# Where the low parts of the merge weights are subtracted, and how fast the convolution is handed out, in a two-layer hybrid block

## The chip, the cores and the metric

The kernel runs on one core of one Trainium2 chip. The metric is the device time of one execution in microseconds (us), as the median of several runs. The engines are TensorE (PE in the profile, its weight loads PEld), VectorE (DVE), ScalarE (ACT), GpSimd (POOL) and SyncE (SP, which here issues nearly all DMA transfers).

## What is computed

The reference is a transformer block of two layers on 1024 tokens of 1024 features, with 256 context tokens ahead of them that are updated in the first layer only. Per layer, one wide product `h @ w_in` yields the inputs of three branches (a: a gated convolution along the sequence, b: neighbourhood attention, c: window attention) and the merge gates. Each branch is gated, projected and weighed by its merge gate:

```python
def conv_branch(u_glu, u_gate, conv_w, conv_b, ln_g, ln_b, w_proj):
    a = u_glu[..., :D_CONV] * jax.nn.sigmoid(u_glu[..., D_CONV:])
    a = depthwise_conv(a, conv_w, conv_b)
    a = jax.nn.silu(layer_norm(a, ln_g, ln_b))
    return (a * jax.nn.silu(u_gate)) @ w_proj
...
    y_a = conv_branch(a_glu, a_gate, conv_w, conv_b, cln_g, cln_b, w_proj_a)
    y_b = (o_na * jax.nn.silu(n_gate)) @ w_proj_b
    y_c = (o_wa * jax.nn.silu(w_gate)) @ w_proj_c
    g_a, g_b, g_c = jnp.split(merge, 3, axis=-1)
    y = jax.nn.sigmoid(g_a) * y_a + jax.nn.sigmoid(g_b) * y_b + jax.nn.sigmoid(g_c) * y_c
    return y @ w_o
```

The depthwise convolution has 31 taps (`CONV_K`) on 512 channels (`D_CONV`). `w_in` has 3 x 1024 columns for the merge gates and 512 for the gate of each branch.

## The kernel before

Everything is held with features on the 128 partitions and tokens along the free axis. The tokens come in groups of 512, 512 and 256 (`GROUPS`; the last is the context). Layer 0 works on all three (`ngr` = 3), layer 1 on the first two. The inputs are 32-bit floats, and each product is made from a high and a low part of weights (`wf`) and of activations (`hh`, `hl`): `product` (L686) issues three matmuls per 128 rows of the contraction, high with high, high weights with the low part of the activations, low weights with the high part. A product over 1024 features is 24 matmuls.

**Weights.** `load_w` (L640) brings half a block, 128 x 512 elements: a DMA from SP into a raw tile `rf` (two of these), a copy on ScalarE for the high part (L649), and a subtraction `rf` less high part for the low part (L650) on the engine that it is given, POOL if nothing is said. `load_block` (L652) makes two halves. There are four tiles `wf`, which is two blocks: a new block can be written only when PE has left the block before the last.

**Stages of a layer.** Norms and input projections, then the attention with other work filled in between, then what is left of the merge gates, the gates of branch b, the projection of b, gates and projections of c and a, and the output pass with `w_o`. The stage of this change begins where the attention ends.

**Merge gates.** `merge_gates` (L881) goes through 24 weight blocks per layer (three branches, eight blocks each). For each block and group of tokens it makes one product into a bank of PSUM (`mg_ps`); ScalarE evicts it through Tanh into `mg_t` (L893) and sends it to DRAM from its own queue. At the end of a block, `merges.load` (L903) starts the load of the block after the next. A part of the first blocks runs within the attention. After it, `merges.wide` is set, the products alternate between two pools of banks, and `along` (L877) pulls the convolution beside them.

**Convolution and its norm.** `side_norm` lists four channel blocks of convolution on 1024 tokens (and four on 256 tokens in layer 0), then the layer norms of all groups in turns. `conv` (L734) is 31 taps on DVE in two chains, `cv_out` (L745, L752) and `cv_odd` (L755, L757), their sum (L759), and a store to DRAM (L760). `conv_norm` (L763) loads a group again (`ln_in`, L772), sums its four channel blocks on DVE (L776, L778), and has PE spread the sum over the partitions with a matrix of ones (L781); DVE subtracts the mean (L783) and adds the squares (L787); PE adds them up in narrow matmuls (L791); DVE makes the reciprocal root and POOL puts it on a diagonal (L799), PE spreads it (L802), DVE multiplies (L804), and the last multiplication (L811) ends the SiLU. `Pace` (L856) hands this generator out: each stretch of products adds its nominal time, multiplied with `SHARE[0]`, to a credit, and steps are taken while the credit lasts.

**Gates of b.** `gate_blocks` (L908) does four weight blocks with one product per group (`gt_ps`), Tanh on ScalarE (L831), a multiplication on DVE (L832), and the product with the branch's output on POOL, ScalarE and POOL (L842 to L844). The same `Pace` goes on beside it, and what it still holds is issued behind the gates (`norming.finish()`). Its weight blocks, and those of the projections, are loaded with the subtraction on POOL.

**What sets the order.** PE's order is the order in which the code issues its instructions (`manual_schedule` for PE). The orders of the other engines and of SP's queue are made by the framework's scheduler from the whole program; each engine then works in that order.

Of the kernel before, what the change touches and what calls it, by code (L numbers as in the profile page):

```python
# [24 lines left out]
NEG = -3.0e38  # L25
FILL_NS = (1975.0, 2300.0)
FIRST_NS = 8000.0
SHARE = (0.9, 0.6)
LOAD_AT = 0
SWITCH_NS = 0.0  # L30
BUILD_AT = ((0, 1), (0, 1))
# [19 lines left out]
def hybrid_block_kernel(  # L51
# [9 lines left out]
    nc = tc.nc  # L61
# [581 lines left out]
    def load_w(src, pw, eng=nc.gpsimd):  # L643

        n = src.shape[1]
        raw = pw.tile([128, 4, 128], F32, tag="rf", bufs=RF, name="rf")
        nc.sync.dma_start(out=raw[:, 0:n, :], in_=src)
        w = pw.tile([128, 2, 4, 128], F32R, tag="wf", bufs=WF, name="wf")
        nc.scalar.activation(w[:, 0, 0:n, :], raw[:, 0:n, :], AF.Copy)  # L649
        eng.tensor_tensor(w[:, 1, 0:n, :], raw[:, 0:n, :], f32(w[:, 0, 0:n, :]), ALU.subtract)  # L650
        return w

    def load_block(src, pw, eng=(nc.gpsimd, nc.gpsimd)):
        return chunks_of([load_w(src[:, 4 * i:4 * i + 4, :], pw, eng[i]) for i in range(2)])
# [34 lines left out]
    def product(w, kn, hx, n, ps):  # L689

        hh, hl = hx
        for k in range(kn):
            for i, (b, a) in enumerate(((0, hh), (0, hl), (1, hh))):
                nc.tensor.matmul(  # L694
                    ps[:, 0:n], lhsT=w(k, b), rhs=a[:, k, 0:n],
                    start=(k == 0 and i == 0), stop=(k == kn - 1 and i == 2),
                )
            if k < kn - 1:
                yield 3 * max(n / 2.4, 107)

    def chunks_of(ws):
        return lambda k, b: ws[k // 4][:, b, k % 4, :]

    def mm_tile(name):
        return ps_mm.tile([128, 512], F32, tag="mm", name=name)
# [3 lines left out]
    def s_tile(name):  # L709
        flip[0] ^= 1  # L710
        if flip[0]:
            return ps_s.tile([128, 1024], F32, tag="s", name=name)
        return ps_t.tile([128, 1024], F32, tag="t", name=name)
# [143 lines left out]
    J0 = {"a": 12, "b": 20, "c": 28}  # L857
# [19 lines left out]
    def along(gen, side):  # L877
        for ns in gen:
            side.pull(ns)

    def merge_gates(l, h, pw, ngr, merges):  # L881


        flip = 0
        while merges.ready:
            br, f, w = merges.ready.pop(0)
            for gi in range(ngr):
                o, n = GROUPS[gi]
                flip ^= 1
                ps = s_tile("mg_ps") if merges.wide and flip else mm_tile("mg_ps")  # L890
                yield from product(w, KC, h[gi], n, ps)
                t = pw.tile([128, 512], F32, tag="t", bufs=3, name="mg_t")
                nc.scalar.activation(t[:, 0:n], ps[:, 0:n], AF.Tanh, scale=0.5)  # L893
                nc.scalar.dma_start(out=mg_d[br][f][:, o:o + n], in_=t[:, 0:n])
                yield 3 * max(n / 2.4, 107)
            merges.load(l, pw)

    class Merges:
# [4 lines left out]
        def load(self, l, pw):  # L903
            if self.todo:
                br, f = self.todo.pop(0)
                self.ready.append((br, f, load_block(wF[l, J0[br] + f], pw)))

    def gate_blocks(l, br, h, pw, px, og, ngr, side):  # L908

# [121 lines left out]
    def side_pool(l, nm, left):  # L1031
        return tc.tile_pool(name=f"{nm}{l}", bufs=1, reuse_waits="tile", side="left" if left == (l == 0) else "right")
# [45 lines left out]
    for l in range(L):  # L1078
# [7 lines left out]
        def end_fill():  # L1086
            spa.close()
            pools["pw"] = sw.enter_context(side_pool(l, "pw", True))
            pools["mg"] = merge_gates(l, h, pools["pw"], ngr, merges)
            merges.load(l, pools["pw"])  # L1090
            merges.load(l, pools["pw"])
            yield END_NS
# [7 lines left out]
        def side_norm():  # L1100
            for c in range(4):
                yield from conv(l, 0, S, c, lc, pools["pc"])
                if ngr == 3:
                    yield from conv(l, S, T, c, lc, pools["pc"])
            yield from in_turns(conv_norm(l, gi, lc, pools["pc"]) for gi in range(ngr))
# [5 lines left out]
        pw = pools["pw"]  # L1111
# [3 lines left out]
        with side_pool(l, "pc", True) as pools["pc"]:  # L1115
            norming = Pace(side_norm(), SHARE[0])
            along(pools["mg"], norming)
# [11 lines left out]
        if l + 1 < L:  # L1129
            cols += [(l + 1, lc_next, j) for j in range(0, 16, 2)]  # L1130
        side = Pace(ada_blocks(cols, px), SHARE[1])
        for br in "bca":
# [144 lines left out]
```

## Time and profile before

| what | value |
|---|---|
| runs | 2892.89, 2867.36, 2889.42 us |
| median | 2889.42 us |
| profiled execution, its own time | 2886.43 us |
| its span, first to last instruction | 2884.6 us |
| mean granted clock of TensorE | 0.98 |
| PE busy in the span | 2722.3 us (94%) |
| DVE, ACT, POOL busy | 1740.0, 1144.6, 1304.2 us |

The profile is of one execution; times in its views are counted from the start of the span. The stage of the change lies at 744.74 to 1100.85 us in layer 0 and at 2242.74 to 2496.40 us in layer 1, and the gates of b right behind it, to 1157 and to 2544 us. "Busy" counts an engine's own work and no waiting. The time in brackets behind a row is the idle time of the engine just ahead of it, with the instruction that released it. The granted clock is a share of TensorE's full speed.

### The profile page before, as it was taken

The numbers are of one execution on the slowest core, as the hardware profiler recorded it, in microseconds if no ns is written. First come the engines' busy times: TensorE is split into PE (matmuls) and PEld (weight loads), VectorE is DVE, ScalarE is ACT, GpSimd is POOL, SyncE is SP. The second block draws the span as 40 slices with busy tenths as digits, with TensorE's granted clock in tenths as the row PEclk, the third lists the DMA queues.
The fourth block names the chain that finished last, engine by engine and source line by source line (L and its number), as shares of the span: only waits on it lengthen the run. The fifth ranks groups of instructions, "written<-read, shape, count | busy, mean of one in ns | idle before, by whom it ended". The sixth has DMA issues, their size and how long they took to land. (4 is left out here: it accounts for less than half of the span.)

```text
span 2884.6 us, 43940 instructions
## 1 busy us (share of the span) xinstructions
PE 2722.3 (94%) x15060; PEld 2361.9 (82%) x15060; DVE 1740.0 (60%) x3676; ACT 1144.6 (40%) x2524; POOL 1304.2 (45%) x1330
## 2 busy tenths in 40 slices
PE   7999999999888999999998899999999995999999
PEld 4899989998777888888877899989888784777877
DVE  5577777766798713786355456677665896441132
ACT  3366666665311124121233356655555221412221
POOL 2333465533565515265645233466334325346652
PEclk9999999999999999999999999999999997999999
DMA  7445442221223323644354455452221332363345
GB/s 240 126 137 149 126 136 67 71 57 48 72 96 130 106 79 118 196 150 133 108 180 157 117 145 158 135 143 71 73 65 63 125 112 87 103 186 107 106 120 175
DMA packets 331664, 344.20 MB, mean 119 GB/s; under 512 B 82224, under 2 KB 249264, under 8 KB 331440
## 3 DMA queue, kind: packets, MB, share of 16 engines
q1 hardware_dynamic: 314160, 313.07, 36.6%
q10 hardware_dynamic: 17280, 28.32, 2.6%
q8 instruction: 119, 1.95, 0.3%
q14 instruction: 105, 0.86, 0.1%
HBM read 250.83 MB, written 90.44 MB: 118 GB/s over the span
## 5 line engine op out<-in xcount | busy, mean ns | idle before, releaser
L650 POOL TENSOR_TENSOR wf<-rf,wf 128x512 fp32r<-128x512 f32 x248 | 479.4, 1937 | 553.1 <-ACT wf L649 538.2
L694 PE MATMUL mg_ps<-hh,wf 128*128 128x512 f32 (+1 forms) x1920 | 574.5, 379 | 60.0 <-POOL wf L650 59.3
L342 PE MATMUL u_ps<-wu,hh 128*128 128x384 f32 (+2 forms) x1920 | 498.9, 342 | 11.4 <-DVE vr L370 3.9
L694 PEld LDWEIGHTS mg_ps<-hh,wf 128*128 128x128 f32 x1920 | 350.2, 190 | 132.6 <-POOL wf L650 62.3
L588 POOL TENSOR_SCALAR p<-p,rd 128x640 f32<-128x640 f32 (+1 forms) x288 | 215.8, 750 | 395.6 <-DVE rd L586 245.4
L694 PE MATMUL mg_ps<-hl,wf 128*128 128x512 f32 (+1 forms) x960 | 358.6, 374 | 0.0
L649 ACT ACTIVATE wf<-rf 128x512 fp32r<-128x512 f32 x272 | 170.4, 627 | 462.1 <-PE pp_ps L694 181.5
L342 PEld LDWEIGHTS u_ps<-wu,hh 128*128 128x128 f32 x1920 | 328.1, 191 | 17.3 <-ACT hh L281 4.7
L342 PE MATMUL u_ps<-wu,hl 128*128 128x384 f32 (+2 forms) x960 | 322.0, 335 | 1.5 <-DVE hl L282 1.2
L580 ACT ACTIVATE p<-p,nmx 128x641 f32<-128x641 f32 (+3 forms) x288 | 222.2, 772 | 245.7 <-DVE nmx L576 122.4
L694 PE MATMUL pp_ps<-ogh,wf 128*128 128x512 f32 (+1 forms) x960 | 282.1, 375 | 5.3 <-DVE mg_in L943 4.0
L694 PE MATMUL gt_ps<-hh,wf 128*128 128x512 f32 (+1 forms) x960 | 280.0, 374 | 5.8 <-DVE mg_in L943 3.4
L598 DVE TENSOR_TENSOR pt<-tp,pt 128x640 fp32r<-128x640 f32 (+1 forms) x288 | 215.8, 749 | 104.8 <-ACT pt L597 101.8
L752 DVE SCALAR_TENSOR_TENSOR cv_out<-cv_in,lc_conv_w,cv_out 128x1024 f32<-128x1024 f32 (+1 forms) x192 | 213.9, 1118 | 0.0
L694 PE MATMUL wo_ps<-hh,wf 128*128 128x512 f32 (+1 forms) x640 | 195.1, 387 | 19.7 <-DVE mg_in L943 7.5
L694 PEld LDWEIGHTS pp_ps<-ogh,wf 128*128 128x128 f32 x960 | 175.3, 189 | 43.3 <-DVE mg_in L943 6.6
L694 PEld LDWEIGHTS mg_ps<-hl,wf 128*128 128x128 f32 x960 | 181.9, 190 | 34.0 <-issue 1.4
L694 PEld LDWEIGHTS gt_ps<-hh,wf 128*128 128x128 f32 x960 | 174.6, 188 | 42.5 <-issue 3.9
L594 PE MATMUL tp<-ident,p 128*128 128x128 f32 x1280 | 187.4, 273 | 14.0 <-DVE pt L598 11.0
L626 POOL TENSOR_TENSOR ob<-cb_b,cb_e 64x256 f32<-64x256 f32 x144 | 106.3, 738 | 200.3 <-ACT cb_e L620 199.8
L597 ACT ACTIVATE pt<-tp 128x640 fp32r<-128x640 f32 (+1 forms) x288 | 181.8, 631 | 17.2 <-PE tp L594 15.1
L594 PEld LDWEIGHTS tp<-ident,p 128*128 128x128 f32 x1280 | 153.6, 140 | 41.1 <-POOL p L588 10.8
(165 smaller groups left out, 5443.1 us busy)
## 6 DMA issues: line engine op xcount, KB each, us to landing
rf<-in_wF SPq DMA_DIRECT2D x144, 256.0 KB, 2.7
rf<-in_wO SPq DMA_DIRECT2D x80, 256.0 KB, 2.9
ru<-in_wU SPq DMA_DIRECT2D x96, 192.0 KB, 3.3
bias<-in_na_bias SPq DMA_DIRECT2D x96, 192.0 KB, 2.6
w_ada_s<-in_w_ada SPq DMA_DIRECT2D x64, 256.0 KB, 3.1
nrm<-qk_d SPq DMA_DIRECT2D x40, 320.0 KB, 3.9
rf<-in_wP SPq DMA_DIRECT2D x48, 256.0 KB, 2.7
v_d<-vr SPq DMA_DIRECT2D x80, 128.0 KB, 2.1
```

What stands on the lines that cost most here:

```text
L342: nc.tensor.matmul(ps[:, c0:UW], lhsT=a[:, k, off * 128:(off + 1) * 128], rhs=ws[k][:, b, c0:UW], start=(k == 0 and i == 0), stop=(k == KC ...
L580: nc.scalar.activation(self.p[:, 0:n], self.p[:, 0:n], AF.Exp, bias=m, scale=1.0 if sink is None else -1.0, accum_out=self.den)
L588: nc.gpsimd.tensor_scalar(p, p, rd, 1.0, ALU.mult, ALU.mult)
L594: nc.tensor.transpose(tp[:, c * 128:(c + 1) * 128], self.p[:, c * 128:(c + 1) * 128], ident)
L597: nc.scalar.activation(self.pt[:, 0:nch, 0, :], tv, AF.Copy)
L598: nc.vector.tensor_tensor(self.pt[:, 0:nch, 1, :], tv, f32(self.pt[:, 0:nch, 0, :]), ALU.subtract)
L626: nc.gpsimd.tensor_tensor(o, b, e, ALU.add)
L649: nc.scalar.activation(w[:, 0, 0:n, :], raw[:, 0:n, :], AF.Copy)
L650: eng.tensor_tensor(w[:, 1, 0:n, :], raw[:, 0:n, :], f32(w[:, 0, 0:n, :]), ALU.subtract)
L694: nc.tensor.matmul(ps[:, 0:n], lhsT=w(k, b), rhs=a[:, k, 0:n], start=(k == 0 and i == 0), stop=(k == kn - 1 and i == 2),)
L752: nc.vector.scalar_tensor_tensor(r, a[:, k:k + n], tap, r, ALU.mult, ALU.add)
```

## The change

`SHARE[0]` goes from 0.9 to 0.8: the convolution and its norms are handed out more slowly against PE's nominal time. In `Merges.load`, blocks that are loaded once `wide` is set, so behind the attention, have their low parts subtracted on VectorE and no more on GpSimd. The weight blocks of the gates, projections and output pass are loaded as before.

```diff
-SHARE = (0.9, 0.6)
+SHARE = (0.8, 0.6)
...
         def load(self, l, pw):
             if self.todo:
                 br, f = self.todo.pop(0)
-                self.ready.append((br, f, load_block(wF[l, J0[br] + f], pw)))
+                eng = nc.vector if self.wide else nc.gpsimd
+                self.ready.append((br, f, load_block(wF[l, J0[br] + f], pw, (eng, eng))))
```

A blank line in `merge_gates` shifts later line numbers by one, and `load` by one more, so that L943 becomes L945.

**DVE, layer 0, merge stage.** The rows of before, some way into the first wide convolution:

```order
L752 SCALAR_TENSOR_TENSOR cv_out<-cv_in,lc_conv_w_400,cv_out 128x1024
L757 SCALAR_TENSOR_TENSOR cv_odd<-cv_in,lc_conv_w_400,cv_odd 128x1024
L752 SCALAR_TENSOR_TENSOR cv_out<-cv_in,lc_conv_w_400,cv_out 128x1024
L757 SCALAR_TENSOR_TENSOR cv_odd<-cv_in,lc_conv_w_400,cv_odd 128x1024
L752 SCALAR_TENSOR_TENSOR cv_out<-cv_in,lc_conv_w_400,cv_out 128x1024
```

The taps of the two chains alternate, and no subtraction stands among them. The rows now, from the first half of one weight block to the first half of the next:

```order
L650 TENSOR_TENSOR wf<-rf,wf 128x512
L752 SCALAR_TENSOR_TENSOR cv_out<-cv_in,lc_conv_w_400,cv_out 128x1024
L650 TENSOR_TENSOR wf<-rf,wf 128x512
L752 SCALAR_TENSOR_TENSOR cv_out<-cv_in,lc_conv_w_400,cv_out 128x1024
L757 SCALAR_TENSOR_TENSOR cv_odd<-cv_in,lc_conv_w_400,cv_odd 128x1024
L752 SCALAR_TENSOR_TENSOR cv_out<-cv_in,lc_conv_w_400,cv_out 128x1024
L757 SCALAR_TENSOR_TENSOR cv_odd<-cv_in,lc_conv_w_400,cv_odd 128x1024
L752 SCALAR_TENSOR_TENSOR cv_out<-cv_in,lc_conv_w_400,cv_out 128x1024
L757 SCALAR_TENSOR_TENSOR cv_odd<-cv_in,lc_conv_w_400,cv_odd 128x1024
L752 SCALAR_TENSOR_TENSOR cv_out<-cv_in,lc_conv_w_400,cv_out 128x1024
L757 SCALAR_TENSOR_TENSOR cv_odd<-cv_in,lc_conv_w_400,cv_odd 128x1024
L752 SCALAR_TENSOR_TENSOR cv_out<-cv_in,lc_conv_w_400,cv_out 128x1024
```

After these the next `L650` row follows. The two subtractions of a block have come into DVE's order, with one tap between them and nine behind them. The pattern holds through the stage of both layers with 8 to 10 wide taps a round in most rounds.

**PE, layer 0, start of the gates of b.** Before, no layer-norm matmul stands there:

```order
L694 MATMUL gt_ps<-hh_418,wf 128x512
L694 MATMUL gt_ps<-hl_419,wf 128x512
L694 MATMUL gt_ps<-hh_418,wf 128x512 x2
L694 MATMUL gt_ps<-hl_419,wf 128x512
L694 MATMUL gt_ps<-hh_418,wf 128x512 x2
L694 MATMUL gt_ps<-hl_419,wf 128x512
L694 MATMUL gt_ps<-hh_418,wf 128x512 x2
```

And now, from the same row on:

```order
L694 MATMUL gt_ps<-hh_418,wf 128x512
L694 MATMUL gt_ps<-hl_419,wf 128x512
L694 MATMUL gt_ps<-hh_418,wf 128x512 x2
L694 MATMUL gt_ps<-hl_419,wf 128x512
L694 MATMUL gt_ps<-hh_418,wf 128x512 x2
L694 MATMUL gt_ps<-hl_419,wf 128x512
L694 MATMUL gt_ps<-hh_418,wf 128x512
L781 MATMUL ln_ps<-ln_s,ones 128x512
L694 MATMUL gt_ps<-hh_418,wf 128x512
```

The first layer-norm matmul of layer 0 has moved from the merge stage to behind the first nine matmuls of the gates; the other sets follow it within the gates, nine in all in layer 0. In layer 1, two sets of L781 and one of L791 move there, and all six now stand in the gates.

**DVE, layer 1, end of the gates of b.** `L832` takes a gate's result; `L811` is the last step of the layer norm. The rows before:

```order
L804 TENSOR_TENSOR ln_in<-ln_in,ln_pr 128x512 x4
L832 SCALAR_TENSOR_TENSOR gt_t<-gt_t,gt_ps 128x512
L811 SCALAR_TENSOR_TENSOR ln_in<-ln_s,ln_in 128x512 x6
L832 SCALAR_TENSOR_TENSOR gt_t<-gt_t,gt_ps 128x512
L811 SCALAR_TENSOR_TENSOR ln_in<-ln_s,ln_in 128x512 x2
L832 SCALAR_TENSOR_TENSOR gt_t<-gt_t,gt_ps 128x512 x5
```

Five of the eight gate results come behind the layer norm's last step. The rows now:

```order
L804 TENSOR_TENSOR ln_in<-ln_in,ln_pr 128x512 x4
L832 SCALAR_TENSOR_TENSOR gt_t<-gt_t,gt_ps 128x512
L804 TENSOR_TENSOR ln_in<-ln_in,ln_pr 128x512 x4
L811 SCALAR_TENSOR_TENSOR ln_in<-ln_s,ln_in 128x512
L832 SCALAR_TENSOR_TENSOR gt_t<-gt_t,gt_ps 128x512
L811 SCALAR_TENSOR_TENSOR ln_in<-ln_s,ln_in 128x512 x6
L832 SCALAR_TENSOR_TENSOR gt_t<-gt_t,gt_ps 128x512
L811 SCALAR_TENSOR_TENSOR ln_in<-ln_s,ln_in 128x512
```

The last `L832` of the gates stands behind six multiplications of the layer norm. The layer norm's end has moved from the third result of the gates to the eighth.

## Rows read from the trace of the kernel before

**Rows 1.** The page, busy time of the engines

```profile
PE 2722.3 (94%) x15060; PEld 2361.9 (82%) x15060; DVE 1740.0 (60%) x3676; ACT 1144.6 (40%) x2524; POOL 1304.2 (45%) x1330
```

**Rows 2.** The page, costliest groups: columns are busy, mean ns, idle before

```profile
L650 POOL TENSOR_TENSOR wf<-rf,wf 128x512 fp32r<-128x512 f32 x248 | 479.4, 1937 | 553.1 <-ACT wf L649 538.2
```

**Rows 3.** Groups of line L650 on DVE: ns min/median/max

```profile
L650 DVE TENSOR_TENSOR wf<-rf,wf x24: 675/691/1643, 1508.2 to 2870.2; 128x512 fp32r<-128x512 f32 x24
```

**Rows 4.** POOL in order of time, quiet parts of both merge stages

```profile
1009.31 1.29 POOL L650 TENSOR_TENSOR wf<-rf,wf 128x512 fp32r<-128x512 f32 x1 [9.93 <-ACT wf L649]
...
1023.31 1.29 POOL L650 TENSOR_TENSOR wf<-rf,wf 128x512 fp32r<-128x512 f32 x1 [11.09 <-ACT wf L649]
...
2447.33 1.29 POOL L650 TENSOR_TENSOR wf<-rf,wf 128x512 fp32r<-128x512 f32 x1 [6.67 <-ACT wf L649]
...
2458.53 1.29 POOL L650 TENSOR_TENSOR wf<-rf,wf 128x512 fp32r<-128x512 f32 x1 [6.67 <-ACT wf L649]
```

**Rows 5.** Table by stretch: merge stage, gates of b; layer 0, then layer 1

```profile
core 0: us, PE busy (x) PEld busy (x) DVE busy (x) ACT busy (x) POOL busy (x), PEclk, DMA share, GB/s
744.74:1100.85 356.11, 328.95 (x1663) 274.73 (x1662) 259.10 (x353) 75.57 (x138) 171.50 (x56) 0.96 0.30 99
1100.85:1157.00 56.15, 56.15 (x291) 47.35 (x290) 15.25 (x21) 21.81 (x43) 34.34 (x29) 1.00 0.38 121
2242.74:2496.40 253.66, 222.47 (x950) 178.19 (x949) 187.89 (x160) 50.41 (x87) 94.50 (x40) 0.94 0.32 106
2496.40:2544.00 47.60, 47.60 (x207) 37.85 (x205) 23.07 (x45) 22.43 (x39) 29.31 (x29) 1.00 0.41 126
```

**Rows 6.** L650 on POOL in layer 0's merge stage, and who waited for it

```profile
L650 POOL TENSOR_TENSOR wf<-rf,wf x44: 1278/1517/26275, 752.0 to 1084.9; 128x512 fp32r<-128x512 f32 x44
...
  PE mg_ps L694: 26.8, 4
```

**Rows 7.** The same in layer 1's merge stage

```profile
L650 POOL TENSOR_TENSOR wf<-rf,wf x39: 1274/1368/33838, 2246.4 to 2493.8; 128x512 fp32r<-128x512 f32 x39
...
  PE mg_ps L694: 31.2, 1
```

**Rows 8.** PE in order of time, the two longest stalls

```profile
844.62 1.22 PE L694 MATMUL mg_ps<-hh,wf 128*128 128x512 f32 x2 [11.26 <-POOL wf L650]
...
2425.75 1.22 PE L694 MATMUL mg_ps<-hh,wf 128*128 128x512 f32 x2 [31.19 <-POOL wf L650]
```

**Rows 9.** POOL in order of time, the two longest pairs

```profile
818.29 28.49 POOL L650 TENSOR_TENSOR wf<-rf,wf 128x512 fp32r<-128x512 f32 x2 [8.35 <-ACT wf L649]
...
2391.85 35.52 POOL L650 TENSOR_TENSOR wf<-rf,wf 128x512 fp32r<-128x512 f32 x2 [17.00 <-ACT wf L649]
```

**Rows 10.** DVE in order of time, layer 0's merge stage

```profile
754.26 2.31 DVE L752 SCALAR_TENSOR_TENSOR cv_out<-cv_in,lc_conv_w,cv_out 128x1024 f32<-128x1024 f32 x1
756.49 1.27 DVE L757 SCALAR_TENSOR_TENSOR cv_odd<-cv_in,lc_conv_w,cv_odd 128x1024 f32<-128x1024 f32 x1
757.68 1.27 DVE L752 SCALAR_TENSOR_TENSOR cv_out<-cv_in,lc_conv_w,cv_out 128x1024 f32<-128x1024 f32 x1
...
797.38 0.47 DVE L757 SCALAR_TENSOR_TENSOR cv_odd<-cv_in,lc_conv_w,cv_odd 128x256 f32<-128x256 f32 x1
797.77 0.47 DVE L752 SCALAR_TENSOR_TENSOR cv_out<-cv_in,lc_conv_w,cv_out 128x256 f32<-128x256 f32 x1
...
1061.91 2.48 DVE L783 SCALAR_TENSOR_TENSOR ln_in<-ln_ps,ln_in 128x512 f32<-128x512 f32 x4 [61.50 <-PE ln_ps L781]
```

**Rows 11.** PE in order of time, layer-norm matmuls in layer 1's merge stage

```profile
2481.37 1.02 PE L781 MATMUL ln_ps<-ln_s,ones 128*128 128x512 f32 x2
...
2482.46 0.39 PE L694 MATMUL mg_ps<-hl,wf 128*128 128x512 f32 x1
...
2494.99 0.95 PE L791 MATMUL ln_ps<-ones,ln_s 128*128 128x1 f32 x8
```

**Rows 12.** DVE in order of time, gates of b in layer 1

```profile
2517.16 3.36 DVE L811 SCALAR_TENSOR_TENSOR ln_in<-ln_s,ln_in 128x512 f32<-128x512 f32 x4 [0.67 <-ACT ln_s L810]
```

## Prediction

> **What bounds the kernel now.** I read the page's totals first. TensorE is busy in 2722.3 of 2884.6 us [rows 1], so time can be won only where TensorE stands still or runs slowly. The costliest group of the page is then the subtraction of the low parts on GpSimd (POOL): 248 of them, 1937 ns each in the mean [rows 2]. The same subtraction takes 0.69 us on VectorE (DVE) where the output pass of this kernel has it there [rows 3], and 1.29 us on POOL where DVE does nothing beside it [rows 4]. So a mean of 1.94 us on POOL must hold some that are far longer.
>
> The table by stretch shows where [rows 5]. The four stretches are, in both layers, what is left of the merge stage after the attention, and the gates of branch b behind it. Layer 0's merge stage takes 356.11 us with PE busy in 328.95 at a granted clock of 0.96, layer 1's 253.66 us with 222.47 busy at 0.94. The gates of b are at full clock and never idle. The waits on the subtraction in these stretches come to 26.8 us in four places in layer 0 and 31.2 us in one place in layer 1, with single subtractions of up to 26.3 and 33.8 us [rows 6, 7]. PE's order of time shows the largest two, 11.26 and 31.19 us, each released by POOL [rows 8]. POOL's order of time shows what happened ahead of them: a pair of subtractions took 28.49 us, another 35.52 us, where a quiet one takes 1.29 [rows 4, 9].
>
> Beside them DVE does the convolution's taps back to back: 1.27 us each, begun 1.19 us apart, and 2.31 us for some that meet a subtraction [rows 10]. All engines but POOL and DVE are idle or light there, so I read a long subtraction as POOL kept out by an unbroken run of taps. DVE has no need of that haste. It has finished its part in layer 0 so early that it waits 61.50 us for PE's first mean of the layer norm [rows 10].
>
> **The change, part by part.** *The low parts move to DVE.* Some 42 subtractions in layer 0 and 36 in layer 1 leave POOL, which then has nothing to do in the merge stage. A weight block is two of them, 24 products per group of tokens. On DVE they cost 2 x 0.61 us of its time per block (0.69 long, taken to overlap its neighbour by the 0.08 us that taps do).
>
> What they meet there decides. DVE works in order, so a subtraction stands behind taps, and taps behind it wait while it waits. A block's buffer comes free when PE leaves the block, the high part follows, and the block is wanted one whole block later. The quiet pairs are 14.00 us apart in layer 0 and 11.20 us in layer 1 [rows 4]: that is PE's time per block, 72 matmuls there and 48 here. From these, a matmul of 512 columns takes 11.20/48 = 0.233 us, and one of 256 takes (14.00 - 11.20)/24 = 0.117.
>
> In the new order 9 taps stand between two pairs and 1 inside a pair. With 1.19 us per wide tap, 0.40 per narrow tap [rows 10] and 0.61 per subtraction, I count 16 rounds of 13.0 to 14.5 us in layer 0, 13.76 in the mean, and 16 rounds of 10.7 us in the mean in layer 1. Both are just under PE's 14.00 and 11.20. DVE is therefore paced by PE, and each pair is ready some 3 us after its buffer is free, 8 to 11 us before PE wants it. In layer 0 the taps run out after these 16 rounds and the last four pairs follow with nothing between. Where the taps were, the subtractions lie beside PE's work, so their cost is nothing; the cover is gone if the taps stretch, which is the third rival.
>
> *What PE gets back.* Layer 0: 22 blocks of 14.00 us, and 45 matmuls (21 of 512 columns, 24 of 256: 7.7 us) are 315.7 us. Nine layer-norm steps of PE stand in that stage, three kinds for three groups. A step of 512 columns costs PE 2482.46 - 2481.37 less the one product between, 0.86 us, and a step of eight small matmuls, recorded with 0.95, some 0.90 by the same reckoning [rows 11]. The narrow group is put at half. That makes 2 x (0.86 + 0.86 + 0.43) for the first and third kind and 0.90 + 0.90 + 0.45 for the second, 6.55 us. Stalls are 26.84. [...] Gain 26.84 + 7.0 = 33.8 us.
>
> Layer 1: 19.5 blocks of 11.20 are 218.4 us, layer-norm steps in that stage 2 x 0.86 + 0.90 = 2.62, stall 31.19; 253.66 less these leaves 1.45 us of low clock. Gain 31.19 + 1.45 = 32.6 us.
>
> *The share of 0.8.* PE's layer-norm matmuls move from the merge stage to the gates of b, all nine sets in layer 0 and three more, so all six, in layer 1. Their PE time moves with them (6.55 and 2.62 us) and nets out to nothing. New is that they are interleaved with gate products, whose results DVE also takes. Layer 1 shows what three such sets do there now: 47.60 us with no idle PE against 192 x 0.233 = 44.8, and 2.6 of layer norm, so 0.1 us per set. By hand, from the durations above, I find no stall of PE in layer 0's gates. In layer 1 the last result of the gates stands behind six multiplications of 0.84 us (four took 3.36 [rows 12]), 5 us of DVE's time, where none stood ahead of it before; by hand, 2.3 us of it are not covered and hold up the projection's first matmuls. From below this costs nothing; from above it is the first rival.
>
> *DMAs.* The weight loads are queued on SP, where the convolution's stores and the layer norm's loads stand too. In the new order a store waits for its last tap, and behind it stand loads whose buffers are freed by a later subtraction anyway; I charge nothing. If one of these did come late by what the longest such wait of DVE costs, the 8 us of lead would take most of it; 5 us per layer is my upper end.
>
> **The sum.** 33.8 + 32.6 - 2.3 = 64.1 us off 2886.43, the profiled execution's own time (its span is 2884.6): 2822 us. That execution is 3 us under the median, 2889.42, so this is 0.977 of the median.
>
> [...] The row is that a subtraction of 1.29 us took up to 33.8 us beside taps of 1.27 us, while many others took little more than 1.3 (median 1.37) [rows 7]. [...]
>
> **The rivals.** *First, the gates give it back.* In the gates of b, DVE must now serve 15 layer-norm sets between the results it takes from PE's two banks. The price at the top is one round of four subtractions of the mean per set, 2.48 us [rows 10]: 15 x 2.48 = 37 us, so 2822 + 37 = 2859. For it: both kinds of result are queued in one order on DVE. Against it: layer 1's three sets stand there now with no PE idle. Chance 0.11.
>
> *Second, no gain: the stalls come from the raw loads.* POOL's pair ahead of layer 1's stall began after 17.00 us of waiting for ScalarE's high part, where 6.67 is usual [rows 4, 9]. If late loads are the cause, the move only changes who waits. Then the 58 us remain and it takes 2886. Against it: those two subtractions then took 35.52 us of their own. Chance 0.05.
>
> *Third, slower: DVE becomes the pacer.* Taps and subtractions now share one order, at 98 and 96% of PE's time per block, 16 x 13.76 + 16 x 10.7 = 391 us against 16 x (14.00 + 11.20) = 403. Should DVE need f times as long, PE is held once 391 f exceeds 403 and the two leads of 11 and 8 us: beyond f = 1.08. At f = 1.24 the whole gain is gone. If every second tap took 2.31 us, as beside POOL now [rows 10], taps (352 of the 391) would grow by 1.43, and the excess is 352 x 1.43 + 39 - 422 = 120 us: 2822 + 120 = 2942. Against it: POOL, which stretches the taps today, has no work in this stage then. Chance 0.03.
>
> **How the numbers follow.** The forecast has 0.81. Its own range is 2803 to 2842: down by what the clock behind small waits elsewhere might give and the spread of an execution (0.3%, 9 us), up by 5 us per layer of late transfers and a half of the gates' price in layer 1. The first rival reaches to 2859, and I set the upper end at 2852, which takes in most of it. Left out are the other two and a part of the first, under 2 in 10 in all. A measurement of this kernel tells about 1% from no change, so faster means under 2860.5 and slower over 2918.3. Faster: 0.81 and all but 0.01 of the first rival, 0.91. Slower: the third, 0.03. Within 1%: the rest, 0.06.
>
> **What would show it.** Right: POOL has no subtraction in the merge stage; each on DVE lasts 0.7 us; PE idles under 3 us there in either layer, at a clock of 0.99 or more; the stage takes some 316 and 218.5 us; the gates of b take 63 us in layer 0 and 50 in layer 1. Wrong: waits of PE on subtractions of DVE; taps in the merge stage still longer than 1.3 us; gates of b over 66 us; or any stall of PE whose releaser is a raw load.

## The result and the profile after

On the chip of the first comparison the changed kernel takes 2840.02 us (2838.72 to 2844.24 in 4 runs) against 2887.77 of the kernel before: a ratio of 0.985, interval 0.980 to 0.990. On a second chip, beside other kernels, it takes 2837.29 against 2902.17, ratio 0.978 (0.976 to 0.980). It is faster, by 48 us in the first case and 65 in the second, where the prediction had 2822 us and a gain of 64. The profiled execution of the changed kernel took 2840.45 us with a span of 2838.6; it is 18.1 us over the forecast span of 2884.6 - 64.1 = 2820.5. The median of 2840.02 us lies inside the forecast range, 2 us under its upper end of 2842.

Where these are is read from the table by stretch of the changed kernel, with the boundaries at the same events as in [rows 5] and one stretch more, from layer 1's projection of b to its output pass (the columns are those of [rows 5]):

```profile
core 0: us, PE busy (x) PEld busy (x) DVE busy (x) ACT busy (x) POOL busy (x), PEclk, DMA share, GB/s
748.30:1065.20 316.90, 316.90 (x1631) 267.12 (x1630) 231.54 (x324) 62.22 (x114) 3.78 (x5) 1.00 0.34 110
1065.20:1133.85 68.65, 64.58 (x322) 52.77 (x322) 47.48 (x92) 34.33 (x65) 36.81 (x38) 0.98 0.29 95
2223.60:2441.80 218.20, 218.20 (x937) 175.52 (x936) 177.27 (x179) 46.07 (x79) 4.61 (x4) 1.00 0.37 123
2441.80:2492.50 50.70, 50.35 (x218) 39.35 (x217) 28.72 (x56) 24.19 (x41) 28.04 (x28) 1.00 0.26 78
2492.50:2742.40 249.90, 231.70 (x977) 184.32 (x976) 77.17 (x118) 55.40 (x94) 135.87 (x106) 0.98 0.46 137
```

Both merge stages have lost their stalls: PE is busy in every microsecond, at a clock of 1.00 where it was 0.96 and 0.94. POOL is left with 4 us of work in each. The gates of b have grown from 56.15 to 68.65 us, and there PE is not busy for 4.07 us of them. Set against the kernel before and the forecast, in us:

| stretch | before | forecast | after | after less forecast |
|---|---|---|---|---|
| merge stage, layer 0 | 356.1 | 315.7 | 316.9 | +1.2 |
| gates of b, layer 0 | 56.1 | 62.7 | 68.65 | +6.0 |
| merge stage, layer 1 | 253.7 | 218.4 | 218.2 | -0.2 |
| gates of b, layer 1 | 47.6 | 50.2 | 50.7 | +0.5 |
| from there to the output pass, layer 1 | 244.5 | 246.8 | 249.9 | +3.1 |
| all other stretches | 1926.6 | 1926.6 | 1934.2 | +7.6 |

The last row is work that the change doesn't touch. In the twelve profiled executions of this study the opening stretch alone took 142.3 to 146.5 us, the attention of layer 0 601.6 to 605.1 and layer 0's output pass 215.9 to 218.9, whatever was changed, and the execution of the changed kernel shown here drew high numbers in two of the three. So of 18 us some 8 look like scatter between executions, and some 10 stand in and behind the gates of b.

The subtractions on DVE, first those of layer 0's merge stage and then of layer 1's (ns of one as min/median/max, and below each what DVE waited for ahead of them):

```profile
L650 DVE TENSOR_TENSOR wf<-rf,wf x42: 675/692/693, 756.7 to 1038.4; 128x512 fp32r<-128x512 f32 x42
...
  ACT wf L649: 57.0, 15
...
L650 DVE TENSOR_TENSOR wf<-rf,wf x36: 678/691/693, 2227.2 to 2420.9; 128x512 fp32r<-128x512 f32 x36
...
  ACT wf L649: 18.6, 15
```

None lasts over 0.69 us, and DVE stood idle 57.0 and 18.6 us ahead of them until ScalarE had written the high part. It waits for a buffer that PE has to free, so PE paces DVE and not the other way round. PE waits for none of them.

The waits of PE that are new, in order of time, two in layer 0's gates of b and two where layer 1's projection of b begins:

```profile
1106.01 1.10 PE L802 MATMUL ln_pr<-ln_s,ones 128*128 128x512 f32 x2 [1.75 <-POOL gt_t L842]
...
1112.91 1.19 PE L802 MATMUL ln_pr<-ln_s,ones 128*128 128x256 f32 x2 [2.31 <-DVE ln_in L804]
...
2500.93 0.50 PE L694 MATMUL pp_ps<-ogh,wf 128*128 128x512 f32 x1 [2.66 <-ACT ogh L843]
2502.28 0.79 PE L694 MATMUL pp_ps<-ogl,wf 128*128 128x512 f32 x1 [0.85 <-POOL ogl L844]
```

In layer 0, `ln_pr`, the matmul that spreads the reciprocal root, waits 1.75 and 2.31 us. The view puts the first of these down to POOL's `L842`, which happens to end at 1105.90. But the diagonal (L799) that this matmul reads was done 7.6 us earlier, at 1098.39. Both waits end 0.15 us after DVE's fourth `L804` of the set before, which still read the bank that the matmul wants (the pool `ps_tr` has a single one). POOL's diagonal, and DVE around the two waits:

```profile
1096.97 1.42 POOL L799 TENSOR_SCALAR ln_s<-ident,n_rstd 128x128 f32<-128x128 f32 x4 [1.35 <-DVE n_rstd L111]
...
1103.39 2.47 DVE L804 TENSOR_TENSOR ln_in<-ln_in,ln_pr 128x512 f32<-128x512 f32 x4
...
1109.69 0.69 DVE L832 SCALAR_TENSOR_TENSOR gt_t<-gt_t,gt_ps 128x512 f32<-128x512 f32 x1 [3.82 <-ACT gt_t L831]
1110.29 2.47 DVE L804 TENSOR_TENSOR ln_in<-ln_in,ln_pr 128x512 f32<-128x512 f32 x4
```

Both rounds of `L804` come late because each stands behind a gate's `L832` in DVE's order. Ahead of the first, three steps of the reciprocal root, 0.16 us each when alone, also took 1.20 to 1.24 us beside three operations of POOL. In layer 1 the projection waits for the last gate's product, which waits for DVE's `L832`. DVE at that place:

```profile
2490.17 2.39 DVE L811 SCALAR_TENSOR_TENSOR ln_in<-ln_s,ln_in 128x512 f32<-128x512 f32 x2
2493.23 5.04 DVE L811 SCALAR_TENSOR_TENSOR ln_in<-ln_s,ln_in 128x512 f32<-128x512 f32 x4 [0.67 <-ACT ln_s L810]
2498.20 0.67 DVE L832 SCALAR_TENSOR_TENSOR gt_t<-gt_t,gt_ps 128x512 f32<-128x512 f32 x1
```

`L832` begins at 2498.20, at the very end of six multiplications of the layer norm. Two of these took 2.39 us and four 5.04, where four took 3.36 before [rows 12]. POOL works without a pause beside these four, on a gate's products and on subtractions of low parts; its operations take 1.68 to 1.75 us each there and 1.26 to 1.31 just before and after.

### The profile page after: what moved, and what is told of

The parts are those of the page before. It is cut to its first block, busy times and chain, and to the rows that moved or that the text cites. A ratio compares the mean times of both kernels' runs of the same rounds, so it can differ in the third digit from the quotient of the medians.

```text
span 2838.6 us, 43932 instructions
## 1 busy us (share of the span) xinstructions
PE 2724.9 (96%) x15060; PEld 2365.3 (83%) x15060; DVE 1746.8 (62%) x3754; ACT 1145.8 (40%) x2524; POOL 1053.6 (37%) x1252
## 5 line engine op out<-in xcount | busy, mean ns | idle before, releaser
L694 PE MATMUL mg_ps<-hh,wf 128*128 128x512 f32 (+1 forms) x1920 | 562.6, 373 | 2.0 <-POOL wf L650 1.3
L650 POOL TENSOR_TENSOR wf<-rf,wf 128x512 fp32r<-128x512 f32 x170 | 226.0, 1331 | 751.9 <-ACT wf L649 743.2
L694 PE MATMUL gt_ps<-hh,wf 128*128 128x512 f32 (+1 forms) x960 | 286.2, 379 | 5.7 <-DVE mg_in L945 3.2
L894 ACT ACTIVATE mg_t<-mg_ps 128x512 f32<-128x512 f32 (+1 forms) x120 | 66.6, 555 | 367.4 <-PE mg_ps L694 362.7
L752 DVE SCALAR_TENSOR_TENSOR cv_out<-cv_in,lc_conv_w,cv_out 128x1024 f32<-128x1024 f32 (+1 forms) x192 | 194.1, 1011 | 0.0
```

Of the source, the lines that this page charges most:

```text
L694: nc.tensor.matmul(ps[:, 0:n], lhsT=w(k, b), rhs=a[:, k, 0:n], start=(k == 0 and i == 0), stop=(k == kn - 1 and i == 2),)
L752: nc.vector.scalar_tensor_tensor(r, a[:, k:k + n], tap, r, ALU.mult, ALU.add)
```

## The experiments

Two questions were open. Why does a subtraction of 1.29 us take 34 us on POOL (a run of taps on DVE keeps it out, or its raw load is late)? And where do the 10 us by the gates come from?

**The share alone.**

```diff
-SHARE = (0.9, 0.6)
+SHARE = (0.8, 0.6)
```

> Share 0.8 alone, the low parts stay on POOL. Theory A (a subtraction on POOL is kept out by an unbroken run of two-input taps on DVE, wherever the run is long): the taps still run back to back, so stalls of PE on POOL's subtraction stay, 20 to 60 us over both merge stages, and the layer-norm sets cost what they cost in the gates of b: 2885 to 2905 us. Theory S (the slower hand-out alone removes the stalls): under 5 us of stalls on POOL, 2840 to 2850 us.

Measured: 2912.43 us (2883.25 to 2927.56 in 10 runs), ratio 1.008 (1.003 to 1.013). Slower by under 1.5%; the median is 7 us over the expectation, and at its upper end (2905.06) if the longest run is left out. PE's waits on POOL's subtraction, in layer 0 and in layer 1 (us in total, times, longest):

```profile
PE mg_ps L694 <- POOL wf L650: 25.7, 4, 10.9
...
PE mg_ps L694 <- POOL wf L650: 29.9, 1, 29.9
```

These are the stalls of [rows 6, 7] again. A slower hand-out removes none of them: 25.7 and 29.9 us of waits, 26.8 and 31.2 before. By the author's reading DVE works its taps as one run however late the code issues them. But the gates of b take 68.6 and 50.7 us here too: this part of the change only costs.

**The low parts alone.** Against the changed kernel:

```diff
-SHARE = (0.8, 0.6)
+SHARE = (0.9, 0.6)
```

> The low parts on DVE, share 0.9 as before. Theory A with G (the moved layer-norm sets cost the changed kernel some 6 us more in layer 0's gates of b than their PE time): no stall on a subtraction, the gates of b 57 us in layer 0 and 48 in layer 1, 2826 to 2834 us. Rival N (the 18 us by which the changed kernel missed the forecast are spread over stages that the change doesn't touch): gates a little shorter, merge stages longer by as much, 2836 to 2844 us. Rival P (at 0.9 DVE paces PE, which the share of 0.8 avoids): PE waits 10 us or more on DVE's subtractions or on the layer norm in the merge stages, over 2845 us.

Measured: 2823.63 us (2818.34 to 2829.01), ratio 0.977 (0.971 to 0.983), a little under the expectation of theory A with G, which holds: gates of 56.0 and 47.4 us. At 0.9 DVE doesn't pace PE; no wait of PE on a subtraction or on the sums is left in the merge stages. To take the chip out of the comparison, both kernels were run again beside each other:

> The changed kernel again, beside share 0.9 on one chip: 2838 to 2846 us, layer 0's gates of b 68 to 69 us, those of layer 1 50 to 51 and the stretch from there to the output pass 249 to 251.

> The low parts on DVE with share 0.9, beside the changed kernel on one chip. If the share of 0.8 costs what the stretches of the profiles say (12.6 + 3.2 us in the gates, 6 behind those of layer 1, less 9.9 us of merge stage): 10 to 17 us under the changed kernel. If that was the chip: within 5 us of it.

Measured: 2837.29 us (2830.76 to 2840.94) for the changed kernel, 2822.27 (2821.58 to 2827.07) with share 0.9, ratios 0.978 (0.976 to 0.980) and 0.973 (0.972 to 0.975) on the same chip. The table by stretch, first of the changed kernel in this comparison, in the order of the one above:

```profile
749.00:1065.90 316.90, 316.90 (x1630) 267.15 (x1630) 231.54 (x324) 62.25 (x114) 3.76 (x4) 1.00 0.33 110
1065.90:1134.60 68.70, 64.66 (x322) 52.85 (x321) 47.52 (x92) 34.33 (x65) 36.75 (x38) 0.98 0.29 94
2220.80:2439.10 218.30, 218.30 (x937) 175.59 (x937) 177.28 (x179) 46.05 (x79) 4.61 (x4) 1.00 0.36 122
2439.10:2489.70 50.60, 50.27 (x218) 39.27 (x217) 28.76 (x56) 24.26 (x41) 28.06 (x28) 1.00 0.25 78
2489.70:2742.80 253.10, 232.96 (x978) 185.58 (x976) 76.26 (x117) 55.29 (x94) 135.87 (x106) 0.97 0.44 135
```

and of the one with share 0.9:

```profile
745.90:1068.50 322.60, 322.27 (x1662) 270.69 (x1661) 258.63 (x395) 75.59 (x138) 6.88 (x14) 1.00 0.33 109
1068.50:1124.60 56.10, 56.10 (x291) 47.30 (x290) 15.20 (x21) 21.74 (x43) 34.25 (x29) 1.00 0.38 121
2210.30:2431.10 220.80, 220.80 (x948) 177.16 (x947) 186.75 (x196) 50.58 (x87) 4.61 (x4) 1.00 0.36 122
2431.10:2478.50 47.40, 47.40 (x205) 37.70 (x204) 22.93 (x44) 22.05 (x38) 29.18 (x28) 1.00 0.39 126
2478.50:2724.30 245.80, 230.81 (x977) 184.39 (x975) 70.45 (x112) 52.28 (x89) 134.05 (x105) 0.98 0.43 131
```

The share of 0.8 costs 68.70 + 50.60 - 56.10 - 47.40 = 15.8 us in the gates, gives back 322.60 + 220.80 - 316.90 - 218.30 = 8.2 in the merge stages (the moved matmuls of the layer norm), and costs 253.10 - 245.80 = 7.3 behind layer 1's gates, 14.9 in all; the times differ by 15.0. The traced executions themselves differ by 19.3 us; the other 4.4 lie in stretches that the share doesn't touch, 3.6 of them in the opening one. The stretch behind the gates is longer here than expected (249 to 251). Of its 7.3 us, 2.1 are the waits of the projection of b on the gates' products (`ogh`, `ogl`), 3.9 us with share 0.8 and 1.8 with 0.9. Another 2.9 are waits on the sums of a further side stream (`ada_sum`, L189) right behind it, with share 0.8 and then with 0.9:

```profile
PE ada_sum L189 <- DVE ada_acc L213: 8.4, 3, 4.0
...
PE ada_sum L189 <- DVE ada_acc L213: 5.5, 3, 3.0
```

The last 2.2 are longer work of PE (232.96 us for 230.81). Over all traced executions this stretch took 248.0 to 253.1 us in the four in which `L832` stands behind the six multiplications, and 243.4 to 245.8 in the seven with a share of 0.9 or 1.0, where it doesn't.

**Breaking the run.** The kernel before, with the loads and POOL's subtractions as they are, and one tiny instruction on DVE after every fourth tap:

```diff
                 nc.vector.scalar_tensor_tensor(odd, a[:, k:k + n], tap, odd, ALU.mult, ALU.add)
+            if k % 4 == 1:
+                nc.vector.tensor_scalar(r[:, 0:1], r[:, 0:1], 1.0, None, ALU.mult)
             yield cost
```

> Kernel before, with one more one-input instruction on DVE (a column of cv_out times 1.0) after every fourth tap, the low parts still on POOL, the loads unchanged. Theory A: POOL gets in at each of these, no subtraction takes longer than 8 us, stalls of PE on it under 5 us in both stages together, 2825 to 2850 us. Theory B (the raw loads are late, or POOL is slow for a reason of its own): stalls as before, 40 to 60 us, 2880 to 2900 us.

Measured: 2837.40 us (2835.04 to 2837.87), ratio 0.983 (0.978 to 0.988). POOL's subtractions, around layer 0's merge stage and around layer 1's:

```profile
L650 POOL TENSOR_TENSOR wf<-rf,wf x55: 1278/1473/2385, 753.4 to 1139.7; 128x512 fp32r<-128x512 f32 x55
...
L650 POOL TENSOR_TENSOR wf<-rf,wf x50: 1273/1330/3352, 2200.8 to 2497.3; 128x512 fp32r<-128x512 f32 x50
```

The longest is 3.4 us, against 26.3 and 33.8 in [rows 6, 7]. PE waits 3.3 us on POOL's subtraction and 4.1 on ScalarE's high part in both stages together, where it waited 58. With not one load moved, 50 us are gone: theory A holds and the late loads (theory B) fall. In the order, the scheduler also puts single narrow taps behind these breaks in layer 0; layer 1, which has none, shows the same.

**Which break, and how often.** The same with a break of two SBUF inputs, the taps' own kind:

```diff
+            if k % 4 == 1:
+                nc.vector.scalar_tensor_tensor(r[:, 0:1], r[:, 0:1], 1.0, r[:, 0:1], ALU.mult, ALU.max)
```

> As the kernel with a break after every fourth tap, with the break now an instruction of two inputs (one column of cv_out, the maximum of itself with itself). Theory A1 (it is the second SBUF input of the taps that keeps POOL out, and only an instruction without one lets it in): subtractions of over 20 us and stalls of 30 to 60 us are back, 2875 to 2905 us. Theory A2 (any short instruction that waits for the tap before it, so any gap in the run, lets POOL in): no subtraction over 8 us, stalls under 8 us, 2830 to 2845 us.

Measured: 2838.62 us (2838.24 to 2844.24), ratio 0.980 (0.978 to 0.982).

```profile
L650 POOL TENSOR_TENSOR wf<-rf,wf x54: 1265/1410/7032, 753.4 to 1135.5; 128x512 fp32r<-128x512 f32 x54
...
L650 POOL TENSOR_TENSOR wf<-rf,wf x50: 1273/1416/7792, 2201.4 to 2499.4; 128x512 fp32r<-128x512 f32 x50
```

A1 falls: a short instruction among the taps lets POOL in, with one input (longest subtraction 3.4 us) or with two (7.8). The 7.8 us are no missed break, since the scheduler left six taps between the two breaks there, from 2301.39 to 2308.56. That the break waits for the tap ahead of it, as A2 has it, isn't seen: 61 of the 96 breaks stand behind a tap of the other chain, which they don't read, and they begin 1.20 us after a wide tap, as the next tap would. PE's waits on POOL are 6.0 us in both stages, and 4.9 on ScalarE's high part. Then the one-input break at every twelfth tap; against the first of these kernels:

```diff
-            if k % 4 == 1:
+            if k % 12 == 1:
```

> The one-input break after every twelfth tap in place of every fourth, the low parts on POOL. Theory A: a subtraction can be kept out for one run, 12 taps of 1.2 us and what narrow taps lie among them, so the longest takes 14 to 18 us and PE, which has a lead of 8 to 11 us, waits some 3 to 8 us at the few that meet a whole run: 5 to 25 us of stalls in all, between the 7 us with every fourth and the 58 us of the kernel before; 2840 to 2870 us. If the length of the run has nothing to do with it: stalls as with every fourth, under 8 us, or as before, over 50.

Measured: 2845.68 us (2844.37 to 2846.08), ratio 0.982 (0.980 to 0.983).

```profile
L650 POOL TENSOR_TENSOR wf<-rf,wf x54: 1278/1436/8976, 757.9 to 1137.1; 128x512 fp32r<-128x512 f32 x54
...
L650 POOL TENSOR_TENSOR wf<-rf,wf x48: 1270/1650/15623, 2202.7 to 2493.6; 128x512 fp32r<-128x512 f32 x48
```

In layer 1 the longest is 15.6 us, one run of twelve taps and its end, as expected; in layer 0, where the longest was issued six taps ahead of a break, it is 9.0. PE waits 10.3 us on POOL. So the longest subtraction follows the length of the run: 33.8 us without breaks, 15.6 with one at every twelfth tap, 3.4 and 7.8 at every fourth. What ends a run in the kernel before can be seen in DVE's order of time, beside the pair of subtractions that began at 818.29 [rows 9]:

```profile
818.25 1.28 DVE L752 SCALAR_TENSOR_TENSOR cv_out<-cv_in,lc_conv_w,cv_out 128x1024 f32<-128x1024 f32 x1
819.44 1.28 DVE L757 SCALAR_TENSOR_TENSOR cv_odd<-cv_in,lc_conv_w,cv_odd 128x1024 f32<-128x1024 f32 x1
...
842.16 1.28 DVE L752 SCALAR_TENSOR_TENSOR cv_out<-cv_in,lc_conv_w,cv_out 128x1024 f32<-128x1024 f32 x1
843.39 0.07 DVE L740 MEMSET cv_in<- 128x15 f32 x1
...
843.48 2.17 DVE L752 SCALAR_TENSOR_TENSOR cv_out<-cv_in,lc_conv_w,cv_out 128x1024 f32<-128x1024 f32 x1
```

The pair was issued 40 ns after a tap had begun, 20 further taps passed at 1.20 us each, and after the first instruction of another kind, a memset of 15 columns, a tap took 2.17 us: the sign that POOL was in. Another kind of instruction alone is not enough. In layer 1's stall, sums of the layer norm and of the convolution went by before POOL got in, beside the last of these:

```profile
2422.15 1.21 DVE L759 TENSOR_TENSOR cv_out<-cv_out,cv_odd 128x1024 f32<-128x1024 f32 x1
2423.29 0.68 DVE L778 TENSOR_TENSOR ln_s<-ln_s,ln_in 128x512 f32<-128x512 f32 x1
2423.89 0.68 DVE L776 TENSOR_TENSOR ln_s<-ln_in 128x512 f32<-128x512 f32 x1
2424.60 1.64 DVE L778 TENSOR_TENSOR ln_s<-ln_s,ln_in 128x512 f32<-128x512 f32 x1
```

It begins 0.71 us after the instruction ahead of it, where 0.60 is usual, so DVE stood still for 0.03 us; and it took 1.64 us for 0.68.

**A run doesn't keep every subtraction out.** In the kernel before, 28 subtractions were issued while a wide tap of 1.27 us ran. Of these, 23 ended within 2.4 us, which is the rest of that tap and their own 1.29. Two of them, in layer 1:

```profile
2268.89 2.11 POOL L650 TENSOR_TENSOR wf<-rf,wf 128x512 fp32r<-128x512 f32 x1 [6.10 <-ACT wf L649]
...
2302.49 2.39 POOL L650 TENSOR_TENSOR wf<-rf,wf 128x512 fp32r<-128x512 f32 x1 [6.43 <-ACT wf L649]
```

The other five took 15.2 to 33.8 us, and the five stalls of PE in [rows 6, 7] are theirs. With the share alone it is 22 and five, and the five stand at the same places of the program. The moment of issue doesn't decide it: 39 ns into a tap led to 26.3 us, 43 ns to 2.39. What does decide it stays open.

**A share of 1.0.** Against the changed kernel:

```diff
-SHARE = (0.8, 0.6)
+SHARE = (1.0, 0.6)
```

> The changed kernel with a share of 1.0. If only the layer-norm sets in the gates of b cost time, nothing more is to be had than at 0.9 (2823.6): 2820 to 2828 us, with all sets of layer 0 and more of layer 1's ahead of the gates. If PE reaches the sums of the convolution before DVE has them, it waits in layer 1's merge stage for ln_s, 3 to 15 us: 2827 to 2840 us.

Measured: 2829.90 us (2825.06 to 2831.80), ratio 0.976 (0.975 to 0.978), on a chip where the kernel before took 2898.09. One wait has come in layer 1's merge stage:

```profile
PE ln_ps L781 <- DVE ln_s L778: 3.3, 1, 3.3
```

The gates of layer 1 fall to 44.8 us, the products alone, and the merge stage grows from 220.8 to 227.3. By the ratios it is not better than 0.9; whether it is worse was not settled, as they ran on different chips.

**The diagonal on ScalarE.** The changed kernel with the multiplication of L799 as an activation:

```diff
-            nc.gpsimd.tensor_scalar(acc[:, j * 128:(j + 1) * 128], ident, r[:, j:j + 1], 1.0, ALU.mult, ALU.mult)
+            nc.scalar.activation(acc[:, j * 128:(j + 1) * 128], ident, AF.Copy, scale=r[:, j:j + 1])
```

> The changed kernel with the diagonal of the layer norm (L799) made on ScalarE in place of POOL, so that it no longer stands behind the gates' multiplications on POOL. If the two waits of PE in layer 0's gates of b (1.8 us on POOL, 2.3 on DVE) are what the moved sets cost: the wait on POOL goes, that on DVE stays or shrinks, gates of b 65 to 67 us in place of 68.6, and the time falls by 2 to 5 us, to 2835 to 2838 us. If ScalarE's queue takes POOL's place: no change, 2838 to 2843 us.

Measured: 2836.33 us (2833.80 to 2849.02), ratio 0.980 (0.977 to 0.982). The gates of b in layer 0, in a table by stretch, and the two waits of PE there:

```profile
1065.00:1132.10 67.10, 63.69 (x322) 51.46 (x321) 47.85 (x92) 37.26 (x75) 33.22 (x28) 1.00 0.31 96
```

```profile
1106.04 1.10 PE L802 MATMUL ln_pr<-ln_s,ones 128*128 128x512 f32 x2 [2.05 <-DVE ln_in L804]
...
1111.39 0.67 PE L802 MATMUL ln_pr<-ln_s,ones 128*128 128x256 f32 x2 [0.77 <-DVE ln_in L804]
```

The first wait stays, 2.05 us for 1.75, now put down to `L804`: the diagonal on POOL was not its cause. The second falls from 2.31 to 0.77, since `L832` and the `L804` behind it come earlier in this order, and the gates take 67.1 us for 68.65, just over the 65 to 67 expected. The 1.5 us are seen in the stretch; the whole time can't show them, since the changed kernel didn't run on this chip.

**The end of layer 1's gates.** The changed kernel with the last multiplication of the SiLU left out in layer 1:

```diff
-            nc.vector.scalar_tensor_tensor(xs[c], acc, 1.0, xs[c], ALU.add, ALU.mult)
+            if l == 0:
+                nc.vector.scalar_tensor_tensor(xs[c], acc, 1.0, xs[c], ALU.add, ALU.mult)
```

> The changed kernel without the last multiplication of the convolution's SiLU (L811) in layer 1, which leaves that factor out of branch a there; the last gate result (L832) stands behind none of them. If these six ahead of it cause the late start of layer 1's projection of b: the waits of the projection on ogh and ogl fall from 4.0 us to under 2, the stretch from the projection to the output pass from 250.0 to 244 to 247 us, and the time by 3 to 6 us, to 2834 to 2838 us. If not: 249 to 251 us there, and no change beyond 2 us.

Measured: 2830.45 us (2826.33 to 2832.62), ratio 0.976 (0.974 to 0.978), 6.8 us under the changed kernel on the same chip, somewhat more than expected. The stretch from the projection to the output pass, and the waits of the projection:

```profile
2485.50:2728.50 243.00, 228.12 (x977) 182.33 (x975) 68.33 (x112) 54.69 (x93) 135.52 (x106) 0.99 0.44 133
```

```profile
PE pp_ps L694 <- POOL ogl L845: 1.3, 1, 1.3
...
PE pp_ps L694 <- ACT ogh L844: 0.3, 1, 0.3
```

243.0 us in place of 249.9 to 253.1: all that this stretch had lost is back once the six multiplications are gone from ahead of `L832`. The edit takes out all eight of layer 1, so it shows what they cost there and not their place alone; for the place speak the kernels with share 0.9, which have all eight and 243.4 to 245.8 us. The waits of the projection of b on ogh and ogl are 1.6 us for 3.9. In the table by stretch, the first 50 us of it have a clock of 0.97, where the two executions of the changed kernel had 0.90 and 0.87; but share 0.9 had 0.90 there as well, so how much is clock stays open.

## Why the prediction was right, and where it was off

*What bounds the kernel.* Right. The long subtractions came from DVE's runs of taps; breaking the runs and moving nothing brought 2837.4 us. The prediction saw that many subtractions beside the taps are short; the trace has 23 of 28 so, and the five that were held made the stalls.

*The low parts to DVE at no cost.* Right. No wait of PE on them, DVE idle ahead of them for 57.0 and 18.6 us, and the merge stages at 316.9 and 218.2 us where the sum had 315.7 and 218.4. The sum's 7.0 and 1.45 us beyond the stalls came back with them. With share 0.9 the merge stages took 322.60 and 220.80 us, 33.5 and 32.9 under [rows 5], which is 6.7 and 1.7 more than the stalls of 26.84 and 31.19. No run shows the 7.0 us by itself as time of a lower clock. Before, the granted clock was 0.50 in the first 2 us behind each of the two longest stalls [rows 8] and 1.00 from 6 us behind them on; without stalls it was 1.00 over both stages.

*The share of 0.8.* Here a term was mis-sized: "nets out to nothing" for the moved sets, less 2.3 us in layer 1. The lower bound, 0.1 us per set from layer 1's old gates, was taken as the value. That row was of three sets whose rounds of four subtractions of the mean, 2.48 us each, were already done. By the two kernels that ran beside each other the twelve sets that moved cost 15.0 us, 1.25 us a set, half way between the bounds of 0.1 and 2.5. The prediction's own sign for this case, gates of b over 66 us in layer 0, came up. In layer 0 the step that failed is "By hand, from the durations above, I find no stall of PE in layer 0's gates": twice a spread waits (1.75 and 2.31 us) for the one bank that DVE's `L804` still reads, because these stand behind gate results. That is what the first rival names, "both kinds of result are queued in one order on DVE". About 2 us more in that stretch are no idle time of PE. Its clock of 0.98 is a small part of them: the kernel without the last multiplication, at 1.00, takes 68.4. In layer 1 the mechanism was the one named, `L832` behind six multiplications, and the wait that it was to cause grew by 2.1 us (between the two kernels run beside each other) or 2.6 (from before to after), for the 2.3 of the sum. But the whole stretch lost 7.3 or 5.4 us: the sum had nothing for the `ada_sum` waits behind it, longer by 2.9 and 1.1, nor for PE's longer work, some 2 us.

*The rest of the miss.* Some 8 us of 18 are in stretches that no edit touches, and vary as much between executions of other kernels here. On the second chip the ratio was 0.978, for a forecast of 0.977; but there the kernel before was slower, so that is no proof that the sum was right. The 0.3% in the forecast's range for the spread of an execution is shown by no run of before, whose first three lay 25.5 us apart, 0.9%. The kernel before itself scattered from 2864.65 to 2905.76 us in 13 runs, and the one with the share alone from 2883 to 2928, while every kernel without long runs against POOL stayed within 16 us. Those 13 runs fall into two groups, six up to 2872.65 and seven from 2887.33 on, while seven runs each on two other chips stay within 10 us. A single subtraction that is held through a run is worth up to 31 us of PE's time [rows 7], so one stall more or less would make such a gap; which executions had which stalls was not traced.

*The rivals.* The first, the gates give it back, was the right one to name and came true by two fifths: 15.0 us of the 37 that it priced. The second, late raw loads, is refuted by the breaks. The third, DVE as the pacer, didn't come: not at 0.8 and not at 0.9; at 1.0 a first wait of 3.3 us for DVE's sums appears.

*Beside a run of taps.* If a subtraction waited for the running tap alone, it would end within 1.27 + 1.29 = 2.56 us, an estimate from [rows 4, 10]. The 23 that ended within 2.4 us agree with it, and so does the median of 1.37 [rows 7]; the five that took 15.2 to 33.8 don't. The longest took 3.4 and 7.8, 15.6 and 33.8 us for breaks at every fourth tap, every twelfth and none. Taps that met a subtraction took 2.17 to 2.31 us for 1.27. Why the next tap went ahead of a subtraction that was waiting is not shown by any run.

## What to carry to other kernels

If POOL's instructions are short in the median and very long at the maximum, look at what DVE does beside the long ones: here a back-to-back run of taps held a subtraction of 1.29 us for up to 33.8, and for 15.6 at most with a break at every twelfth tap. Move the urgent operation to DVE, into its order, or break the run every few instructions; on one chip the first brought 64 us and the second 50, and the first, with nothing else changed, was the best kernel of the study (2822.27 us). Don't slow a side stream down in the same step unless its tail has been followed into the next stage, the banks of PSUM included: there its work stood behind evictions in DVE's order and cost 1.25 us per set. And don't take the releaser that a view names for the cause where its end and another's fall together; look for what the waiting instruction reads and writes.

## What the runs showed of the hardware that was not expected

A tiny instruction among the taps lets POOL in even if it has two SBUF inputs itself (longest subtraction 7.8 us for 33.8), so the number of inputs of the breaking instruction is not the point. No gap is to be seen ahead of these breaks either, and a narrow tap of 0.47 us is not short enough: eight of them in a row went by while a subtraction issued at 859.56 in the kernel before was held. In layer 1's stall a full-length sum let POOL in, behind a gap of 0.03 us; so more than one thing can end the hold. And a subtraction that POOL started 40 ns into a tap was held through 20 further taps, 26.3 us, while 23 of 28 ended within 2.4 us, the rest of the running tap and their own 1.29.
